# Fewer slots per expert rank, and one more expert in the one-tile form, in a mixture-of-experts decoder layer

## The chip, the cores and the metric

One core of one Trainium2 chip runs the whole layer in one launch. The metric is the device time of one execution in microseconds (us), as the median of repeated runs. All matrix products go through TensorE (PE), which multiplies a stationary block of at most 128 x 128 by a moving block of up to 512 columns; VectorE (DVE) and ScalarE (ACT) do the elementwise work, GpSimd (POOL) issues the gathers and scatters, and SyncE (SP) issues the other loads.

## The reference

A decoder layer on 1024 tokens of width 1024: gated and dilated attention mixers, a first LayerNorm that gives `h`, then a mixture of 32 experts of which each token takes its 4 best, and a second LayerNorm. The change concerns the mixture alone:

```python
logits = jnp.dot(hf, w_router) + b_router
top_vals, top_idx = lax.top_k(logits, TOP_K)          # 4 of 32
gates = jax.nn.softmax(top_vals, axis=-1)
# for the tokens xb of expert e:
g = jnp.minimum(xb @ w_gate[e] + b_gate[e], SWIGLU_LIMIT)
u = jnp.clip(xb @ w_up[e] + b_up[e], -SWIGLU_LIMIT, SWIGLU_LIMIT)
act = (u + 1.0) * (g * jax.nn.sigmoid(SWIGLU_ALPHA * g))
y[tok] += (act @ w_down[e] + b_down[e]) * gate
```

1024 tokens x 4 make 4096 token-expert pairs; how many of them an expert gets is known only once the router has run. Evaluated on the drawn inputs, the reference's router gives these counts, sorted: 225, 207, 188, 173, 171, 168, 163, 161, 148, 142, 139, 133, 126, 125, 125, 125, 122, 121, 119, 116, 113, 110, 109, 104, 100, 93, 93, 92, 90, 83, 62, 50.

## The kernel before, in words

The kernel computes mixers, first LayerNorm and router in a front stage of some 560 us. The router's part writes, for each expert, a list of tokens and gates into `table` (L632), and `rank()` sorts the experts by their count: rank 0 is the fullest expert, rank 31 the emptiest. The number of tokens is not known when the program is built, so each rank has a fixed number of **slots**, `CAPS[r]` (L42); slots that no token fills point at dummy rows. What does not fit is left over: `left_over()` (L128 to L165) counts, on the chip, the blocks of 128 tokens beyond the slots, and a loop behind the expert stage (L981 to L1039) runs one block per turn, with all twelve weight pieces of that expert loaded again. With no left-over block the loop's body does not run.

The expert stage takes the ranks in the order `ORDER` (L43): 0, 30, 15, 29, 1, 28, 14, 27, 2, 26, 13, 25, 3, 24, 12, 23 and so on to 7, 16, 8, 31. That is a full rank, one of 128 slots, one that is just over 128, one of 128 slots, four by four. Each expert has twelve weight pieces of 1 MB (128 x 2048 float32): eight for gate and up, four for down. `load` (L778) fetches a piece into one of `RAWS` = 5 buffers on SP's queue, ACT rounds it to the high part `wh` (L120) and DVE subtracts to get the low part `wl` in bfloat16 (L121), four pairs of which can stand ready (`SPLITS`). SP's order is written by hand: `pieces` (L795 to L799). The order of the other engines comes from the scheduler, which places each instruction when its inputs are expected.

For each piece PE multiplies high by high, high by low and low by high. There are two forms, by the number of slots n:

- **one-tile** (n of 128 or 64; `gate_up`, `tokens_still`, L821): the tokens are stationary (`xt`, `xbt`; `at`, `abt` for down), the weights move, 512 columns at a time. A piece takes 8 matmuls of 512 columns against `wh` and 4 against `wl`. The bias comes in by one matmul more (L844).
- **wide** (n over 128; `gate_up_wide`, `weights_still`, L830): the weights are stationary, and the tokens move. A piece takes 16 matmuls of 2n columns (`xw` or `aw`, high and low part side by side) and 16 of n columns (`xbw` or `abw`). ACT copies half of each result out of the bank (`sb`, L865 and L918), DVE adds the other half (`tw`, L867 and L919); for down, 16 transposes (L930) turn the result back.

Before an expert starts, `fetch` (L731) gathers its tokens into `xg` (L749, one transfer per 128 slots), and `prepare` (L763) transposes them on PE (L758) and splits them into `xt` and `xbt`, or `xw` and `xbw` (hi on ACT L120, lo on DVE L121, bfloat16 on ACT L760). The pool has one `xt` and one `xw`. The driver of the stage interleaves three things per expert: first half of gate and up, the down of the expert before, `prepare` of the next, second half:

```python
gu(b, 0, lambda: next(extra, None))
...
if last is not None:
    finish = down(last)
if nxt is not None:
    prepare(nxt)
gu(b, 1, lambda: (finish(), turn(b, 0)))
```

`turn` transposes the activations of a one-tile expert for its down product. The tail (L1047 to L1069) is the second LayerNorm.

Of the kernel before, what the change touches and what calls it, by code (L numbers as in the profile page):

```python
# [38 lines left out]
MAGIC = 0x5F3759DF  # L39


CAPS = [256, 240, 216, 208, 192, 184, 176, 168, 160, 152, 152, 144, 144, 140, 136, 136] + [128] * 15 + [64]  # L42
ORDER = [r for n in range(8) for r in (n, 30 - 2 * n, 15 - n, 29 - 2 * n)][:31] + [31]  # L43
MAXOV = 64
AHEAD = 2
# [11 lines left out]
def constants():  # L57
# [15 lines left out]
        "c_row": np.tile(np.arange(MAXOV, dtype=np.float32), (E, 1)),  # L73
        "c_caps": np.array(CAPS, np.float32)[:, None],
    }


def layer(tc, i, out):
# [630 lines left out]
    with (tc.tile_pool(name="c", bufs=1, reuse_waits="tile") as C,  # L709
# [20 lines left out]
        def fetch(r):  # L730
            b = Job()  # L731
            b.r, b.n = r, CAPS[r]
            b.wide = b.n > P
# [390 lines left out]
```

## Time and profile before

| | us |
|---|---|
| median of 3 runs (1987.77 to 1990.61) | 1988.18 |
| the profiled execution, its own time | 1989.86 |
| its span in the trace | 1988.0 |
| expert stage, first token transpose to last weight matmul | 568.5 to about 1944 |

The span is the time between the first and the last instruction; 1.86 us lie around it. "Busy" counts the time in which an engine executes; the chain of waits follows the work that ended last back from the end, and a window gives the busy time of each engine between two times. The TensorE clock that the chip granted (PEclk) is a share of full speed.

### The profile page before, as it was taken

The numbers are of one execution on the slowest core, as the hardware profiler recorded it, in microseconds if no ns is written. First come the engines' busy times: TensorE is split into PE (matmuls) and PEld (weight loads), VectorE is DVE, ScalarE is ACT, GpSimd is POOL, SyncE is SP. The second block draws the span as 40 slices with busy tenths as digits, with TensorE's granted clock in tenths as the row PEclk, the third lists the DMA queues.
The fourth block names the chain that finished last, engine by engine and source line by source line (L and its number), as shares of the span: only waits on it lengthen the run. The fifth ranks groups of instructions, "written<-read, shape, count | busy, mean of one in ns | idle before, by whom it ended". The sixth has DMA issues, their size and how long they took to land.

```text
span 1988.0 us, 32785 instructions
## 1 busy us (share of the span) xinstructions
PE 1864.2 (94%) x12402; PEld 1549.6 (78%) x12484; DVE 1563.0 (79%) x2195; ACT 1331.1 (67%) x1761; POOL 314.3 (16%) x202
## 2 busy tenths in 40 slices
PE   8999999989859999999999999999999999999981
PEld 7788786678747878887888888888888888888861
DVE  5754656667758887797879888888988988888895
ACT  5534525643247877687778778778877887877873
POOL 2111110213320111020112101011111110111110
PEclk9999999989979999999999999999999999999996
DMA  5111101242278898799789889999999999999884
GB/s 201 50 43 35 50 25 38 64 141 99 83 255 307 303 354 272 271 327 353 292 291 373 300 318 324 367 319 312 369 318 319 364 315 341 332 355 338 300 286 175
DMA packets 92657, 495.94 MB, mean 249 GB/s; under 512 B 20264, under 2 KB 20824, under 8 KB 43344
## 3 DMA queue, kind: packets, MB, share of 16 engines
q1 hardware_dynamic: 76128, 442.49, 60.3%
q0 software_dynamic: 14064, 42.92, 8.9%
q10 hardware_dynamic: 2304, 8.39, 1.1%
q8 instruction: 100, 1.64, 0.3%
q14 instruction: 61, 0.50, 0.1%
HBM read 457.04 MB, written 36.72 MB: 248 GB/s over the span
## 4 chain that ended last, share of the span: by engine, by line
PE 60%; DMA 4%; DVE 4%; issue 2%; ACT 2%; POOL 0%; SPq 0%; POOLq 0%; ACTq 0%; DVEq 0%
PE b L830 32%; PE b L821 23%; DMA raw<-in_w_moe 2%; PE b L758 2%; DVE wl L121 2%; PE b L930 1%; ACT wh L120 1%; DMA ys<-o,tg 1%; PE b L844 1%; DVE y L1069 1%; DVE y L1068 0%; DMA y<-ys 0%; DMA table<-pay,dst 0%; POOL table L632 0%; DMA xg<-hs,tg 0%
## 5 line engine op out<-in xcount | busy, mean ns | idle before, releaser
L121 DVE TENSOR_TENSOR wl<-raw,wh 128x2048 bf16<-128x2048 f32 (+1 forms) x385 | 874.9, 2284 | 151.1 <-ACT wh L120 149.8
L120 ACT ACTIVATE wh<-raw 128x2048 fp32r<-128x2048 f32 (+1 forms) x394 | 742.4, 1893 | 143.8 <-PE b L821 37.9
L830 PE MATMUL b<-xw,wh 128*128 128x272 f32 (+12 forms) x2048 | 352.4, 325 | 0.0
L830 PEld LDWEIGHTS b<-xw,wh 128*128 128x128 f32 x2048 | 319.1, 188 | 12.3
L821 PE MATMUL b<-wh,xt 128*128 128x512 f32 x992 | 267.6, 411 | 0.0
L830 PEld LDWEIGHTS <-wl 128*128 128x128 bf16 x3072 | 225.6, 98 | 19.0 <-issue 5.5
L821 PEld LDWEIGHTS b<-wh,xt 128*128 128x128 f32 x992 | 188.5, 190 | 47.5
L749 POOL DMA_INDIRECT xg<-hs,tg x48 | 78.7, 1639 | 791.1 <-PE b L758 353.4
L830 PE MATMUL b<-aw,wh 128*128 128x272 f32 (+12 forms) x1024 | 174.2, 325 | 0.0
L933 POOL DMA_INDIRECT ys<-o,tg x48 | 111.9, 2332 | 390.5 <-ACT o L931 152.8
L830 PE MATMUL b<-xbw,wl 128*128 128x136 bf16 (+12 forms) x2048 | 166.1, 239 | 0.7 <-DVE wl L121 0.7
L830 PEld LDWEIGHTS b<-aw,wh 128*128 128x128 f32 x1024 | 159.5, 188 | 6.2
L865 ACT ACTIVATE sb<-b 128x136 f32<-128x136 f32 (+12 forms) x256 | 78.2, 317 | 90.8 <-PE b L830 84.6
L821 PE MATMUL b<-wh,at 128*128 128x512 f32 x496 | 137.7, 419 | 0.0
L821 PE MATMUL b<-wl,xbt 128*128 128x512 bf16 x465 | 116.0, 380 | 2.9 <-issue 0.2
L821 PEld LDWEIGHTS b<-wh,at 128*128 128x128 f32 x496 | 93.1, 190 | 24.4 <-issue 0.6
L867 DVE SCALAR_TENSOR_TENSOR tw<-b,bias,sb 128x136 f32<-128x136 f32 (+12 forms) x256 | 91.5, 393 | 15.8 <-ACT sb L865 14.8
L821 PEld LDWEIGHTS <-xbt 128*128 128x128 bf16 x512 | 45.0, 98 | 63.2 <-issue 18.1
L830 PE MATMUL b<-abw,wl 128*128 128x136 bf16 (+12 forms) x1024 | 83.3, 239 | 2.5 <-DVE wl L121 2.5
L918 ACT ACTIVATE sb<-b 128x136 f32<-128x136 f32 (+12 forms) x128 | 38.5, 315 | 59.5 <-PE b L830 50.8
L124 PE MATMUL mm<-xh,wh 128*128 128x512 f32 x160 | 67.9, 424 | 10.3 <-DVE ks L359 6.9
L124 PE MATMUL mm<-vh,xh 128*128 128x256 f32 x256 | 72.6, 284 | 0.6 <-DVE ql L344 0.6
(364 smaller groups left out, 2842.1 us busy)
## 6 DMA issues: line engine op xcount, KB each, us to landing
raw<-in_w_moe SPq DMA_DIRECT2D x384, 1024.0 KB, 7.2
raw<-in_w_in SPq DMA_DIRECT2D x18, 512.0 KB, 3.6
raw<-in_w_out SPq DMA_DIRECT2D x8, 512.0 KB, 3.7
t<-in_x SPq DMA_DIRECT2D x8, 512.0 KB, 4.0
hs<-pt ACTq DMA_DIRECT2D x8, 512.0 KB, 3.1
ys<-pr ACTq DMA_DIRECT2D x8, 512.0 KB, 2.6
y<-ys SPq DMA_DIRECT2D x8, 512.0 KB, 5.7
out<-y SPq DMA_DIRECT2D x8, 512.0 KB, 2.6
```

The lines of the kernel that those rows point to most:

```text
L120: S.activation(hi, src, AF.Copy)
L121: by.tensor_tensor(lo, src, hi.bitcast(FT), op=OP.subtract)
L124: TE.matmul(o, ah, bh, start=start, stop=False)
L749: k.got = G.indirect_dma_start(out=k.x[:k.n], out_offset=None, in_=hs, in_offset=bass.IndirectOffsetOnAxis(ap=k.idx, axis=0))
L758: TE.transpose(tp[:, j], src(j), ident[:n, :n])
L821: TE.matmul(o, a, b, start=first and q == 0, stop=kq == 1 and q == len(every) - 1)
L830: TE.matmul(o, a, b, start=kq == 0 and j == 0, stop=kq == 1 and j == 3)
L844: TE.matmul(p, b.oh, bhl[:, m, half * 512:half * 512 + 512], start=True, stop=False)
L865: S.activation(x2[:, :n], p[f][:, n:2 * n], AF.Copy)
L867: V.scalar_tensor_tensor(t[:, f * n:f * n + n], p[f][:, :n], b.bias[:, c:c + 1], x2[:, :n], op0=OP.add, op1=OP.add)
L918: S.activation(x2[:, :n], p[:, n:2 * n], AF.Copy)
L933: G.indirect_dma_start(out=ys, out_offset=bass.IndirectOffsetOnAxis(ap=k.idx, axis=0), in_=k.o[:k.n], in_offset=None, compute_op=OP.add)
```

## The change

The list of slots per rank gets smaller numbers, and the sixteenth rank goes from 136 to 128, which by the test `b.n > P` makes it one-tile:

```diff
-CAPS = [256, 240, 216, 208, 192, 184, 176, 168, 160, 152, 152, 144, 144, 140, 136, 136] + [128] * 15 + [64]
+CAPS = [256, 220, 208, 196, 184, 176, 168, 164, 156, 148, 144, 140, 140, 136, 132, 128] + [128] * 15 + [64]
```

Nothing else differs. The scheduler then orders PE, ACT and DVE anew. Two places follow.

**ACT, second half of gate and up of a rank just over 128 slots.** `sb` is the copy out of the banks, `wh` the split of a weight piece, `aw` and `abw` the split of the activations, `t` the gate function of the one-tile expert around it. Before, rank 14, with 136 slots:

```order
L865 ACTIVATE sb<-b 128x136 x4
L120 ACTIVATE wh<-raw 128x2048 x3
L120 ACTIVATE aw<-tw 128x4x136
L880 ACTIVATE abw<-tw 128x544
L705 ACTIVATE t<-b 128x512
L120 ACTIVATE wh<-raw 128x2048 x3
L918 ACTIVATE sb<-b 128x136 x4
```

Now rank 14, with 132 slots:

```order
L865 ACTIVATE sb<-b 128x132
L120 ACTIVATE wh<-raw 128x2048 x2
L705 ACTIVATE t<-b 128x512
L120 ACTIVATE wh<-raw 128x2048
L120 ACTIVATE aw<-tw 128x4x132
L880 ACTIVATE abw<-tw 128x528
L120 ACTIVATE wh<-raw 128x2048 x2
L918 ACTIVATE sb<-b 128x132 x4
```

And now rank 13, with 136 slots:

```order
L865 ACTIVATE sb<-b 128x136 x4
L120 ACTIVATE wh<-raw 128x2048 x3
L120 ACTIVATE aw<-tw 128x4x136
L880 ACTIVATE abw<-tw 128x544
L705 ACTIVATE t<-b 128x512
L120 ACTIVATE wh<-raw 128x2048 x3
L918 ACTIVATE sb<-b 128x136 x4
```

At rank 14 the gate function and one weight split stand ahead of `aw`; at rank 13 the row order is the one that ranks 15 and 14 had before: three weight splits, `aw`, `abw`, and the gate function behind them.

**PE and DVE, from rank 30 (one-tile) to rank 15.** The last matmuls of rank 30's second half read `xt_5590`. On PE before, rank 15 follows with its own wide tile `xw_6101`, filled ahead:

```order
L821 MATMUL b_6207<-wl_6158,xbt_5591 128x512
L821 MATMUL b_6207<-wh_6157,xt_5590 128x512 x8
L830 MATMUL b_6266<-xw_6101,wh_6211 128x272 x4
L830 MATMUL b_6267<-xw_6101,wh_6211 128x272 x4
L830 MATMUL b_6268<-xw_6101,wh_6211 128x272 x4
L830 MATMUL b_6269<-xw_6101,wh_6211 128x272 x4
```

Now rank 15 is one-tile, and its tokens go into a second tenant of the one `xt` buffer, `xt_6096`:

```order
L821 MATMUL b_6188<-wh_6138,xt_5590 128x512 x8
L844 MATMUL b_6247<-bhl_5298,oh_6114 128x512
L149 MATMUL b_6285<-vc_5476,lt32_168 32x2
L844 MATMUL b_6294<-bhl_5298,oh_6114 128x512
L821 MATMUL b_6247<-wh_6192,xt_6096 128x512
L821 MATMUL b_6294<-wh_6251,xt_6096 128x512
L821 MATMUL b_6247<-wh_6192,xt_6096 128x512 x7
L821 MATMUL b_6294<-wh_6251,xt_6096 128x512
```

On DVE the split that fills it now stands there:

```order
L121 TENSOR_TENSOR at_5815<-b_6180,at_5815 128x4x128
L121 TENSOR_TENSOR wl_6252<-raw_6249,wh_6251 128x2048
L121 TENSOR_TENSOR xt_6096<-b_6098,xt_6096 128x4x128
L121 TENSOR_TENSOR xt_6096<-b_6106,xt_6096 128x4x128
L706 TENSOR_SCALAR t_6228<-b_6188 128x512
L121 TENSOR_TENSOR wl_6270<-raw_6267,wh_6269 128x2048
L707 SCALAR_TENSOR_TENSOR act_6226<-t_6227,t_6228 128x512
```

Between the last read of `xt_5590` and the first of `xt_6096` PE has two bias matmuls (and a small one of `left_over`); on DVE the two halves of `xt_6096` stand behind a weight split. The same pattern follows at the next passage, from rank 15 to rank 29. Before, the kernel had no passage from one 128-slot expert to another.

## Rows read from the trace of the kernel before

**Rows 1.** The page: busy time of each engine; the chain of waits by line.

```profile
PE 1864.2 (94%) x12402; PEld 1549.6 (78%) x12484; DVE 1563.0 (79%) x2195; ACT 1331.1 (67%) x1761; POOL 314.3 (16%) x202
...
PE b L830 32%; PE b L821 23%; DMA raw<-in_w_moe 2%; PE b L758 2%; DVE wl L121 2%; PE b L930 1%; ACT wh L120 1%; DMA ys<-o,tg 1%; PE b L844 1%; DVE y L1069 1%; DVE y L1068 0%; DMA y<-ys 0%; DMA table<-pay,dst 0%; POOL table L632 0%; DMA xg<-hs,tg 0%
```

**Rows 2.** Windows per pair: us; busy of PE, PEld, DVE, ACT, POOL; PEclk, DMA, GB/s.

```profile
652.10:729.20 77.10, 76.06 (x586) 63.79 (x589) 66.38 (x74) 62.76 (x75) 13.14 (x6) 1.00 0.94 329
729.20:834.30 105.10, 101.89 (x577) 82.56 (x580) 82.80 (x73) 72.37 (x82) 10.95 (x6) 0.98 0.82 288
834.30:911.40 77.10, 75.13 (x577) 63.33 (x580) 65.39 (x65) 62.59 (x75) 13.22 (x6) 1.00 0.95 327
911.40:1010.40 99.00, 96.09 (x579) 81.60 (x582) 81.21 (x73) 71.02 (x82) 10.97 (x6) 0.98 0.85 306
1010.40:1086.90 76.50, 76.17 (x578) 64.48 (x581) 68.02 (x66) 64.76 (x78) 16.20 (x6) 1.00 0.96 336
1086.90:1179.70 92.80, 92.32 (x579) 79.69 (x581) 77.50 (x72) 69.03 (x78) 9.51 (x6) 1.00 0.88 321
...
1347.00:1424.40 77.40, 77.08 (x579) 65.33 (x581) 68.41 (x66) 65.06 (x78) 11.56 (x6) 1.00 0.96 343
...
1676.20:1755.70 79.50, 79.22 (x579) 67.32 (x582) 70.08 (x66) 66.18 (x78) 12.75 (x6) 1.00 0.96 345
```

**Rows 3.** Groups by shape, TensorE: line, out<-in, shape, count; busy us, mean ns.

```profile
L830 PE MATMUL b<-xw,wh 128*128 128x272 f32 x256 | 35.4, 291 | 0.0
...
L830 PE MATMUL b<-xw,wh 128*128 128x480 f32 x128 | 29.0, 381 | 0.0
...
L830 PE MATMUL b<-xbw,wl 128*128 128x136 bf16 x256 | 16.5, 223 | 0.0
...
L830 PE MATMUL b<-xbw,wl 128*128 128x240 bf16 x128 | 13.8, 266 | 0.0
```

**Rows 4.** Windows, four weight pieces each: one-tile form, then wide form of 136.

```profile
618.70:630.50 11.80, 11.75 (x52) 7.86 (x52) 11.36 (x13) 10.07 (x8) 0.00 (x0) 1.00 0.63 239
667.60:679.90 12.30, 12.30 (x131) 11.97 (x131) 12.23 (x17) 10.01 (x12) 2.78 (x1) 1.00 0.96 296
```

**Rows 5.** Timeline of TensorE: start, us, what; sixteen token transposes.

```profile
729.15 1.81 PE L758 MATMUL b<-ident,xg 128*128 128x128 f32 x16
```

**Rows 6.** Waits of TensorE in the expert stage: total us, times, longest us.

```profile
PE b L844 <- DVE tw L919: 6.7, 4, 2.8
```

**Rows 7.** Timeline of ScalarE at rank 15: start, us, what [idle before <-releaser].

```profile
714.71 1.92 ACT L120 ACTIVATE wh<-raw 128x2048 fp32r<-128x2048 f32 x1 [2.79 <-DMA raw<-in_w_moe]
716.53 0.64 ACT L120 ACTIVATE aw<-tw 128x544 fp32r<-128x544 f32 x1
```

**Rows 8.** Windows just behind the wait after rank 15, and in a stretch of fast loads.

```profile
735.00:745.00 10.00, 9.78 (x49) 7.19 (x50) 7.83 (x7) 8.30 (x12) 0.95 (x1) 0.86 0.95 350
1083.00:1093.00 10.00, 9.71 (x82) 8.12 (x81) 10.00 (x15) 8.92 (x14) 0.17 (x1) 1.00 1.01 415
```

**Rows 9.** Waits of ScalarE for weight loads, ranks 15, 11, 10: us, times, longest.

```profile
ACT wh L120 <- DMA raw<-in_w_moe: 6.9, 4, 3.3
...
ACT wh L120 <- DMA raw<-in_w_moe: 3.4, 2, 2.8
...
ACT wh L120 <- DMA raw<-in_w_moe: 2.2, 1, 2.2
```

**Rows 10.** Groups by shape, VectorE, expert stage.

```profile
L121 DVE TENSOR_TENSOR wl<-raw,wh 128x2048 bf16<-128x2048 f32 x380 | 864.7, 2287 | 151.1 <-ACT wh L120 149.8
...
L121 DVE TENSOR_TENSOR xt<-b,xt 128x512 fp32r<-128x512 f32 x30 | 19.3, 680 | 0.0
```

**Rows 11.** Groups by shape, ScalarE, expert stage.

```profile
L120 ACT ACTIVATE xt<-b 128x512 fp32r<-128x512 f32 x30 | 16.4, 600 | 0.1
```

**Rows 12.** DMA issues of the whole run: count, KB each, median us to landing.

```profile
raw<-in_w_moe SPq DMA_DIRECT2D x384, 1024.0 KB, 7.2
...
ys<-o,tg POOLq DMA_INDIRECT x48, 9.9
```

## The prediction

> **What bounds the kernel now.** I read the page first [rows 1]: PE is busy for 94% of the span, and the chain of waits runs for 55% through the weight matmuls of the two forms, L830 (wide) and L821 (one-tile). A busy share says little of what one slot costs, so I went to windows. I cut the expert stage where the token transposes of a wide expert begin, so that each window holds one wide expert and one one-tile expert, twelve weight pieces of each [rows 2]; in order these are the pairs of ranks 15, 1, 14, 2, 13, 3, 11 and 9, with 136, 240, 136, 216, 140, 208, 144 and 152 slots. Three things are to be seen. First, in the pairs of 13, 3, 11 and 9 PE idles for 0.3 to 0.5 us in 76.5 to 92.8: PE's own work sets the time there. Second, the pairs of 15, 1, 14 and 2 have 1.0 to 3.2 us of idle PE; the list of PE's waits names DVE's `tw` in front of the bias matmul L844, 6.7 us in 4 waits, 2.8 the longest [rows 6]. Third, the DMA share is 0.94 to 0.96 in the pairs just over 128 slots and 0.82 to 0.88 in those of the full ranks. PE leads, the loads are close behind it, and DVE (66.4 of 77.1 us) and ACT come after.
>
> **Fewer slots in the wide form.** A wide piece has 16 matmuls of 2n columns and 16 of n. From 272 to 480 columns the mean goes from 291 to 381 ns, 0.433 ns per column; from 136 to 240 in bfloat16 from 223 to 266 ns, 0.413 ns [rows 3]. One slot costs 16 x (2 x 0.433 + 0.413) = 20.5 ns per piece, and 12 pieces make 0.2455 us. The windows agree: from 144 to 208 slots a pair grows from 77.4 to 92.8 us, 0.241 us per slot [rows 2]. Ranks 1 to 14 lose 20, 8, 12, 8, 8, 8, 4, 4, 4, 8, 4, 4, 4 and 4 slots, 100 in all: **-24.6 us**. The copies, adds and splits on ACT and DVE and the gathers of the second parts shrink too; I cost that at nothing, as PE's matmuls hide them. If that cover went, DVE with 66.4 us and ACT with 62.8 would still be below the 71 to 75 us that the shortest pair will have.
>
> **Rank 15 in the one-tile form.** Four pieces take 12.3 us wide with 136 slots and 11.8 us one-tile, biases included [rows 4]; three times that is 1.5 us. The wide expert also has 16 transposes of its result and 16 of its tokens against 8 and 8, and sixteen take 1.81 us [rows 5]. Together **-3.3 us**. A gather and a scatter of 8 rows on POOL's queue and a bias load on SP's go as well, all off the path.
>
> **The wait behind rank 15.** On the line of 0.2455 us per slot from rank 11's 77.4 us, a pair with 136 slots should take 75.4; it takes 77.1. Rank 1's pair should take 92.8 + 32 x 0.2455 = 100.7; it takes 105.1. So 1.7 + 4.4 = 6.1 us are lost at rank 15, and by the same sum 1.7 + 4.2 = 5.9 at rank 14. The pair of rank 13, 76.5 us, is on the line (76.4). Why: ACT's timeline at rank 15 shows a weight split that waits 2.79 us for its load and the split `aw` behind it [rows 7]; DVE then runs late, its `tw` comes behind two weight splits of 2.29 us, and PE waits for banks. Just behind that wait the granted clock of a 10 us window is 0.86, so part of it ran at 1.2 instead of 2.4 GHz [rows 8]; that is in the 4.4. With rank 15 one-tile there is no `aw` and no `tw` at that place: **-6.1 us**.
>
> **Ranks 14 and 13.** The loss stands where ACT has three weight splits, `aw`, and the gate function last, and not at rank 13, where the gate function and another split stood ahead. The change gives rank 14 the good row and rank 13, now at 136 slots, the bad one. So I let 5.9 us go at rank 14 and come back at rank 13: **0**.
>
> **The passages 30 to 15 and 15 to 29.** New: one `xt` buffer for two one-tile experts in a row. The split into it can't begin before PE has read the old tokens for the last time, and PE has only two bias matmuls meanwhile. No row shows this wait. With idle engines it is an ACT half and a DVE half, 0.60 + 0.68 = 1.3 us [rows 10, 11], less the two bias matmuls of 512 columns, 0.413 x 512 = 0.21 each [rows 3]: 0.9. On DVE a weight split of 2.29 us stands in front, which could begin just before: 2.29 + 0.68 - 0.42 = 2.5. Queued behind these are ACT's next weight split and DVE's gate chain, which have a piece or two of lead. I take 1.5 each, since ACT's part of the weight split ahead is free to run some two us before the passage: **+3.0 us**, ends 1.8 and 5.0.
>
> **The loads come nearer.** ACT waits 2.2 us for weight loads in rank 10's pair (152 slots), 3.4 in rank 11's (144), 6.9 in rank 15's [rows 9]: about 0.3 us per slot less. The ranks 9 to 14 lose 28 slots, so 8.2 us more of such waits. In rank 11's pair nothing of it reached PE, in rank 15's most; I take a quarter, **+2.0 us**, ends 0 and 8.2.
>
> **Sum.** -24.6 - 3.3 - 6.1 + 0 + 3.0 + 2.0 = -29.0 us. The profiled execution took 1989.86 us (span 1988.0 and 1.86 around it) and would take 1960.9; the median of the runs stands 1.68 lower, and I forecast **1959.2 us**.
>
> **Rivals.**
>
> *The loads set a floor under the pairs just over 128 slots.* If no pair gets under the shortest seen, 76.5 us, rank 15 gives 0.6, rank 14 0.6, rank 13 nothing, ranks 12 and 11 0.8 and 0.9, rank 10 2.0 and rank 9 1.0, together 5.9; the 72 slots of the ranks 1 to 8 give 17.7; the waits stay. That is -23.6: 1964.6 us. For it: the DMA share of 0.96. Against it: 10 us windows that moved 415 GB/s while PE stood at 9.7 of 10 [rows 8], where the best pair has a mean of 345. The Trainium skill (DMA: Bandwidth & Descriptors, section "Where 436 GB/s comes from") says that for transfers between HBM and SBUF the HBM side binds, at about 358 GB/s; by that, a pair's 27.4 MB (345 GB/s x 79.5 us) would need 76.6 us, the same floor. The 415 GB/s of the window speak against it.
>
> *The passages cost their upper end and the clock.* 2.5 us each and, as behind the 2.8 us wait, 14% of 10 us at the lower clock, 1.4 us: 2 x 3.9 = 7.8 in place of 3.0, 1964.0 us.
>
> *No wait at rank 13 either, and the loads keep up.* The gathers for rank 2 and rank 3 are smaller than those that followed ranks 15 and 14. Then 5.9 + 2.0 us more go: 1951.3 us.
>
> *Rank 14 keeps its wait though its row is better,* because PE comes even sooner there: 5.9 us less gain, 1965.1 us.
>
> *Slower: one expert overflows.* All rests on counts under the new slots. The reference's router gives 225, 207, 188, 173, 171, 168, 163, 161 for the ranks 0 to 7 against 256, 220, 208, 196, 184, 176, 168, 164; the tightest is rank 7 with 3 to spare, and the kernel rounds otherwise than the reference. Before, the loop's body did not run: all 384 loads of `w_moe` are the 12 x 32 of the experts [rows 12]. One block would load twelve pieces again with nothing beside it: at least 12 x 2.29 (DVE) + 7.2 + 9.9 = 44.5 us, at most 12 x (7.2 + 2.29) + 9.9 = 124 us [rows 10, 12]; I put it at 65, for three buffers overlap the loads: 2024 us. A single token over decides, since even 44.5 is more than 29.0. The same would hold if the inputs timed were of another drawing.
>
> **The numbers.** Forecast 0.50; the load floor 0.15; the passages 0.10; no waits 0.15; rank 14 keeps its wait 0.07; overflow 0.03. A range from 1951 to 1968 us takes in all of them but the overflow, and the ends of the unknown terms one at a time; some 0.15 may lie outside. A measurement of this kernel can tell about 0.2% (4 us) from no change: faster 0.96, within it 0.01, slower 0.03.
>
> **What would show it.** The pair of rank 3, now 196 slots, at 89.9 us and that of rank 10 (144) at 77.5 confirm the slot price. The window of rank 15's pair should be near 74.5 us (two one-tile experts of some 36 and the waits), with two PE waits of 0.9 to 2.5 us whose releaser is DVE's or ACT's `xt`; rank 1's pair near 95.7, without a wait for `tw`. At rank 13's pair and the one behind it a wait for `tw` of some 2.8 us and a dip of the clock; none at rank 14. No loads beyond 384. I would be wrong if the pairs just over 128 slots stopped at 76.5 us, if PE's waits for `wl` spread over the pairs of ranks 9 to 12, or if anything of L981 to L1039 ran.

## The result and the profile after

The changed kernel takes **1972.26 us** (median of 4 runs, 1969.78 to 1975.34) against 1987.97 for the kernel before, timed beside it: a ratio of 0.9913, 95% interval [0.9898, 0.9929]. That is 15.7 us faster where 29.0 were forecast, and 4.3 us above the upper end of the range, 1968. The profiled execution took 1973.29 us (span 1971.4), 12.4 more than the 1960.9 of the prediction's sum.

The page, busy time and the chain of waits by line, against [rows 1]:

```profile
PE 1844.5 (94%) x12232; PEld 1519.5 (77%) x12232; DVE 1548.3 (79%) x2169; ACT 1315.8 (67%) x1731; POOL 312.1 (16%) x200
...
PE b L830 28%; PE b L821 22%; DMA raw<-in_w_moe 4%; DVE wl L121 3%; DMA ys<-o,tg 3%; PE b L758 2%; ACT wh L120 2%; PE b L930 1%; PE b L844 1%; DVE y L1069 1%; DMA bias<-in_b_guT 0%; DVE y L1068 0%; DMA y<-ys 0%; POOL table L632 0%; DVE tw L867 0%
```

PE is 19.7 us less busy, and the loads of the weights have gone from 2% to 4% of the chain. The windows of the pairs of ranks 15, 1, 14, 2, 13, 3 and 11, cut and laid out as in [rows 2]:

```profile
651.90:721.90 70.00, 69.43 (x329) 47.24 (x328) 55.62 (x48) 51.66 (x46) 10.16 (x5) 1.00 0.93 316
721.90:828.10 106.20, 102.24 (x589) 84.56 (x588) 86.17 (x73) 75.08 (x81) 12.18 (x5) 0.97 0.84 309
828.10:908.40 80.30, 76.34 (x583) 64.23 (x581) 64.88 (x65) 62.06 (x75) 13.01 (x6) 0.98 0.91 316
908.40:1001.90 93.50, 92.53 (x582) 79.60 (x581) 79.86 (x74) 70.56 (x82) 9.52 (x6) 1.00 0.90 321
1001.90:1078.10 76.20, 75.55 (x582) 63.38 (x581) 64.45 (x62) 61.70 (x74) 13.19 (x6) 1.00 0.97 329
1078.10:1173.30 95.20, 91.52 (x583) 78.04 (x582) 80.21 (x76) 70.82 (x83) 11.80 (x6) 0.98 0.87 318
...
1338.80:1415.30 76.50, 76.41 (x582) 64.45 (x580) 67.58 (x66) 64.41 (x78) 12.01 (x6) 1.00 0.97 343
```

The first two have to be read as one. The token transposes that cut them come earlier within rank 15's down product than they do elsewhere, so two of its weight pieces lie in the second window (48 matmuls that read `at` there, 32 in the window of rank 2). Together they take 176.2 us, 182.2 before and 74.5 + 95.7 = 170.2 by the forecast. Rank 14's pair has become longer, 80.3 us with 132 slots where it took 77.1 with 136. Behind rank 13 the window of rank 3 has 3.7 us of idle PE and a clock of 0.98, as forecast. From rank 12 on the pairs lie within 1.2 us of the forecast.

What PE waited for in the expert stage, with `tw` first as in [rows 6] (the list also has 14.3 us at the first gather and 5.3 at the last expert, where the kernel before has 14.4 and 5.0):

```profile
PE b L844 <- DVE tw L919: 6.0, 5, 3.7
PE b L821 <- ACT abt L760: 5.7, 3, 4.0
...
PE b L830 <- DVE wl L121: 2.9, 3, 2.2
PE b L830 <- ACT abw L880: 1.7, 1, 1.7
```

The wait for `tw` has not gone; others have joined it. The longest of those shown lies at rank 1. TensorE's timeline there, and ScalarE's just before:

```profile
721.90 1.68 PE L758 MATMUL b<-ident,xg 128*128 128x128 f32 x16
727.53 1.89 PE L821 MATMUL b<-wl,abt 128*128 128x512 bf16 x4 [3.96 <-ACT abt L760]
```

```profile
712.12 1.91 ACT L120 ACTIVATE wh<-raw 128x2048 fp32r<-128x2048 f32 x1 [2.62 <-DMA raw<-in_w_moe]
...
715.40 1.91 ACT L120 ACTIVATE wh<-raw 128x2048 fp32r<-128x2048 f32 x1 [0.89 <-DMA raw<-in_w_moe]
720.36 1.92 ACT L120 ACTIVATE wh<-raw 128x2048 fp32r<-128x2048 f32 x1 [3.05 <-DMA raw<-in_w_moe]
722.18 0.57 ACT L120 ACTIVATE at<-b 128x512 fp32r<-128x512 f32 x1
722.65 1.90 ACT L120 ACTIVATE wh<-raw 128x2048 fp32r<-128x2048 f32 x1
725.09 1.91 ACT L120 ACTIVATE wh<-raw 128x2048 fp32r<-128x2048 f32 x1 [0.53 <-DMA raw<-in_w_moe]
726.90 0.58 ACT L760 ACTIVATE abt<-b 128x512 bf16<-128x512 f32 x1
```

ACT stands four times for a weight piece that has not landed, 7.1 us in all. Small work that PE needs, `at` and `abt`, is queued behind those splits, and PE stops for 3.96 us. The name in the list of waits is `abt`; what was late is the load (e7 and e10 below). Windows of 10 us around that stretch, columns as in [rows 8]:

```profile
660.00:670.00 10.00, 9.58 (x45) 6.34 (x44) 7.27 (x7) 8.92 (x13) 1.82 (x1) 1.00 0.98 286
670.00:680.00 10.00, 10.00 (x48) 6.63 (x47) 9.32 (x11) 7.59 (x8) 1.84 (x1) 1.00 0.97 287
680.00:690.00 10.00, 9.96 (x49) 6.59 (x48) 9.43 (x7) 6.18 (x6) 0.00 (x0) 1.00 1.00 417
...
720.00:730.00 10.00, 6.04 (x32) 4.00 (x31) 7.93 (x6) 8.30 (x9) 0.00 (x0) 0.81 0.98 389
730.00:740.00 10.00, 10.00 (x39) 6.59 (x38) 5.10 (x7) 7.12 (x9) 2.92 (x1) 0.85 0.65 230
```

Two things show. In 660 to 680, where POOL issues a scatter into `ys` in each window, the DMA engines are as busy as in 680 to 690 (share 0.97 to 1.00) and move 287 instead of 417 GB/s. And in the window of PE's stop and the one behind it the granted clock is 0.81 and 0.85: part of these 20 us ran at 1.2 GHz, the lower of the two levels.

At rank 14 it is DVE that stands, for the tiny load of the bias, 5.64 us, and then PE; the rows of DVE and of PE:

```profile
876.42 0.17 DVE L741 TENSOR_SCALAR bias<-bias 128x8 f32<-128x8 f32 x1 [5.64 <-DMA bias<-in_b_guT]
876.53 2.29 DVE L121 TENSOR_TENSOR wl<-raw,wh 128x2048 bf16<-128x2048 f32 x1
```

```profile
878.88 1.18 PE L830 MATMUL b<-xbw,wl 128*128 128x132 bf16 x16 [2.22 <-DVE wl L121]
```

### The profile page after: what moved, and what is told of

Same layout as the page of the kernel before. It is cut to its first block, busy times and chain, and to the rows that moved or that the text cites. A ratio compares the mean times of both kernels' runs of the same rounds, so it can differ in the third digit from the quotient of the medians.

```text
span 1971.4 us, 32268 instructions
## 1 busy us (share of the span) xinstructions
PE 1844.5 (94%) x12232; PEld 1519.5 (77%) x12232; DVE 1548.3 (79%) x2169; ACT 1315.8 (67%) x1731; POOL 312.1 (16%) x200
## 4 chain that ended last, share of the span: by engine, by line
PE 53%; DMA 8%; DVE 6%; issue 2%; ACT 2%; POOL 1%; SPq 0%; POOLq 0%; ACTq 0%; DVEq 0%
PE b L830 28%; PE b L821 22%; DMA raw<-in_w_moe 4%; DVE wl L121 3%; DMA ys<-o,tg 3%; PE b L758 2%; ACT wh L120 2%; PE b L930 1%; PE b L844 1%; DVE y L1069 1%; DMA bias<-in_b_guT 0%; DVE y L1068 0%; DMA y<-ys 0%; POOL table L632 0%; DVE tw L867 0%
## 5 line engine op out<-in xcount | busy, mean ns | idle before, releaser
L120 ACT ACTIVATE wh<-raw 128x2048 fp32r<-128x2048 f32 (+1 forms) x394 | 742.4, 1893 | 153.0 <-DMA raw<-in_w_moe 46.8
L830 PE MATMUL b<-xw,wh 128*128 128x280 f32 (+13 forms) x1920 | 326.4, 324 | 0.0
L830 PEld LDWEIGHTS b<-xw,wh 128*128 128x128 f32 x1920 | 297.8, 190 | 9.5
L821 PE MATMUL b<-wh,xt 128*128 128x512 f32 x1056 | 283.4, 409 | 0.1
L830 PEld LDWEIGHTS <-wl 128*128 128x128 bf16 x2880 | 209.0, 97 | 18.1 <-issue 5.1
L830 PE MATMUL b<-aw,wh 128*128 128x280 f32 (+13 forms) x960 | 160.0, 321 | 0.7 <-DVE aw L121 0.7
L830 PE MATMUL b<-xbw,wl 128*128 128x140 bf16 (+13 forms) x1920 | 153.4, 237 | 2.2 <-DVE wl L121 2.2
L865 ACT ACTIVATE sb<-b 128x140 f32<-128x140 f32 (+13 forms) x240 | 71.8, 313 | 79.1 <-PE b L830 72.4
L821 PEld LDWEIGHTS b<-wh,at 128*128 128x128 f32 x528 | 99.9, 192 | 26.2 <-issue 0.6
L867 DVE SCALAR_TENSOR_TENSOR tw<-b,bias,sb 128x140 f32<-128x140 f32 (+13 forms) x240 | 83.8, 389 | 11.3 <-ACT sb L865 10.6
L830 PE MATMUL b<-abw,wl 128*128 128x140 bf16 (+13 forms) x960 | 77.1, 237 | 2.4 <-ACT abw L880 1.7
L821 PE MATMUL b<-wl,abt 128*128 128x512 bf16 x272 | 72.4, 390 | 6.2 <-ACT abt L760 5.7
```

The source lines that it names most:

```text
L120: S.activation(hi, src, AF.Copy)
L821: TE.matmul(o, a, b, start=first and q == 0, stop=kq == 1 and q == len(every) - 1)
L830: TE.matmul(o, a, b, start=kq == 0 and j == 0, stop=kq == 1 and j == 3)
L865: S.activation(x2[:, :n], p[f][:, n:2 * n], AF.Copy)
L867: V.scalar_tensor_tensor(t[:, f * n:f * n + n], p[f][:, :n], b.bias[:, c:c + 1], x2[:, :n], op0=OP.add, op1=OP.add)
```

## The experiments

Each kernel's time is a median, with the ratio to the kernel before in the same batch (in 20, 7, 7, 11 and 9 runs of it its median was 1989.2, 1988.7, 1988.4, 1988.7 and 1990.1). From e5 on, theory A means late weight loads and theory B the order of the rows. The first four expectations name their theories otherwise, each in its own words; the theory B of e3 is not the later one.

**One part of the change alone (e1, e2).**

```diff
-CAPS = [256, 220, ... 136, 132, 128] + ...
+CAPS = [256, 220, ... 136, 132, 136] + ...      (e1: rank 15 stays wide)
-CAPS = [256, 240, ... 140, 136, 136] + ...
+CAPS = [256, 240, ... 140, 136, 128] + ...      (e2: from the kernel before, rank 15 alone)
```

> The changed kernel with rank 15 back at 136 slots, in the wide form; all other slots as changed. Theory L (the weight loads fall behind over three one-tile experts in a row, and what the one-tile form gains is given back as a wait in the pair of rank 1): the pair of rank 15 takes 77 us again (70.1 changed), the pair of rank 1 falls from 106 to 96 to 100 us, and the median is within 3 us of the changed kernel's 1972.3. Theory R (the one-tile form of rank 15 is worth its whole price, and the loss in the pair of rank 1 has another cause): the pair of rank 1 stays near 106 us and the median rises by 6 to 9 us, to 1978 to 1981.

> The kernel before with nothing but rank 15 at 128 slots, one-tile. Theory L: the pair of rank 15 falls from 77.1 to 70 us and the pair of rank 1 rises from 105.1 to 109 to 112 us: the median is 1984 to 1988. By the sum of the prediction (3.3 for the form, 6.1 for the wait, less 3.0 for the passages) it is 1981.6, with the pair of rank 1 at 100.7 us.

e1: 1977.51 us, 0.9946 [0.9927, 0.9965]. e2: 1987.81 us, 0.9991 [0.9976, 1.0005]. The slots alone give some 11 us of their 24.6, the form alone nothing that can be told from zero, though on top of the slots it gives some 5 us (1977.5 to 1972.3, in two batches). No theory has all its numbers: e1's time is near theory R's, but rank 1's pair takes 102.2 us, between the two; e2's time is in theory L's range, but rank 1's pair takes 106.1, short of its 109. In e2's profiled execution, at 1983.7 us one of its faster ones, the pairs of 15 and 1 fall from 182.2 to 176.8 us, and rank 2's rises from 99.0 to 100.1. In the changed kernel, with 20 slots less at rank 1, the same two pairs take 176.2. So twenty slots, 4.9 us of PE's work, brought 0.6 there. Something else than PE set the time.

**The bias on another engine, and another order (e3, e4).**

```diff
-                V.tensor_scalar(b.bias[:, 8:], b.bias[:, 8:], 1.0, None, op0=OP.add)
+                G.tensor_scalar(b.bias[:, 8:], b.bias[:, 8:], 1.0, None, op0=OP.add)
```

```diff
-ORDER = [r for n in range(8) for r in (n, 30 - 2 * n, 15 - n, 29 - 2 * n)][:31] + [31]
+ORDER = [0, 30, 15, 1, 29, 14, 28, 2, 27, 13, 26, 3, 25, ... 19, 9, 18, 16, 7, 17, 8, 31]
```

> The changed kernel with the addition of 1 to the bias of a wide expert (L741) on GpSimd in place of VectorE; the other rows of VectorE and all of ScalarE's and TensorE's stand as they did. Theory B (at rank 14 VectorE stands 5.6 us in front of this tiny addition, whose load comes late, and everything behind it in its queue is late): the pair of rank 14 falls from 80.2 to 75 to 76 us, no wait of VectorE for that load is left, and the median is 1966 to 1968. Rival (the weight loads are late there anyway): the pair stays at 79 to 80 us and the median at 1971 to 1973.

> The changed kernel with another order of the experts: rank 15 stands between rank 30 and rank 1, so that two one-tile experts in a row come twice (30, 15 and 18, 16) and three never; full ranks and those just over 128 slots still take turns. Theory L: the wait of 4.0 us and the slow clock behind it at rank 1 go, and the median is 1962 to 1967. Rival (a wait of this kind comes wherever ScalarE has a late weight split in front of the activations): it reappears at other places and the median stays within 3 us of 1972.3.

e3: 1975.32 us, 0.9927 [0.9895, 0.9959]; e4: 1969.37 us, 0.9907 [0.9881, 0.9933]: neither can be told from the changed kernel. In e3 DVE no longer waits for the bias, rank 14's pair falls by 2.0 us to 78.3, and rank 12's rises by 5.0 to 82.5. In e4 the wait for `abt` at rank 1 goes (1.7 us in all are left of 5.7), but `tw` (6.2), `wl` (2.9) and `abw` (2.6) stay. Both moved the loss; neither removed it.

**Loads and scatters taken away (e5 to e8).** e5 is the changed kernel again, for comparison. In e6 and e7 half of each weight piece is not loaded (the first half is used twice), in e6 for the six experts around ranks 1 and 14, in e7 for all but ranks 0 and 30. In e8 the scatters of the ranks 0 to 5 are left out. So e6 to e8 no longer compute the layer and tell about time alone. PE and ACT keep their rows in all of them.

```diff
-            w = SP.dma_start(out=raw, in_=i["w_moe"][ds(e, 1), c].rearrange("a p c -> p (a c)"))
+            w = SP.dma_start(out=raw[:, 0:2] if r in HALF else raw, in_=i["w_moe"][ds(e, 1), c][:, :, 0:1024 if r in HALF else 2048].rearrange("a p c -> p (a c)"))
...
-            split(h, l, raw)
+            split(h, l, raw) if r not in HALF else split(*(z.rearrange("p (a b) c -> p a (b c)", a=2) for z in (h, l)), raw[:, 0:2].rearrange("p b c -> p (b c)").unsqueeze(1).to_broadcast([P, 2, 1024]))
```

```diff
+                if b.r < 6:
+                    return
                 for k in b.parts:
                     G.indirect_dma_start(out=ys, ...
```

> The changed kernel itself, timed beside the three others of this batch, so that they can be compared with it on one chip. Both theories expect what it did before: some 1972 us, rank 1's pair near 106 us and rank 14's near 80, where the slot line gives 95.7 and 74.6. If these losses wander to other pairs from one profiled execution to the next, they depend on when loads land and not on the row order alone.

> Left out: the second half of every weight piece of the experts 15, 29, 1, 28, 14 and 27 is not loaded, the first half is read twice by the splits in its place. ACT and PE have the very same row order as the changed kernel, on DVE the bias add moves by one weight split at two places. Theory A (weight loads land late beside gathers and scatters, and the in-order queues hand the delay on): the loss of 10.4 us in rank 1's pair and of 5.6 in rank 14's goes, so 106.2 becomes about 96 and 80.2 about 75, the total falls by some 15 us to about 1957, and the loss at rank 13 or 3 stays. Theory B (the order of rows on ACT and DVE makes PE wait, loads or not): the two pairs stay within 2 us of 106 and 80 and the total within 4 us of the changed kernel.

> Left out: as before, now for all experts but 0 and 30, so that weight loads take half of their traffic nearly everywhere. Theory A: besides the 15 us at ranks 1 and 14, the waits for tw behind rank 13 (4 us) and what the loads took from the later pairs (1 us each in the pairs of 15 to 9) go: 1948 to 1953 us, with no wait of PE over 2 us between the first and the last expert. Theory B: within 4 us of the changed kernel; the wait for tw behind rank 13, which stands at the row order with the gate function behind aw, stays at 3 to 4 us in any case if the row order makes it.

> Left out: the scatter-add of the results of the ranks 0 to 5 (11 transfers of up to 128 rows of 4 KB, read, add and write), the order on PE, ACT and DVE is unchanged. If theory A holds and the scatters of the full ranks are the traffic that delays the weight loads, the pairs of ranks 1 and 14 lose 5 to 12 of their 16 us of delay and the total falls to 1958 to 1967. If the weights alone fill the queues there, the pairs stay within 2 us and the total within 4 us of the changed kernel. Theory B expects no change either.

e5: 1974.33 us (0.9923), with the losses in the same places: rank 1's pair 106.4 us, rank 14's 80.2. e6: 1963.46 us, 0.9866 [0.9841, 0.9891], 10.9 below e5. e7: 1952.81 us, 0.9823 [0.9807, 0.9839], 21.5 below. e8: 1963.47 us, 0.9874 [0.9858, 0.9891], 10.9 below. The windows of the pairs of ranks 15, 1, 14 and 3 in e7:

```profile
652.40:722.50 70.10, 69.01 (x324) 47.31 (x329) 59.23 (x52) 54.93 (x49) 10.92 (x5) 1.00 0.74 218
722.50:822.30 99.80, 99.29 (x585) 83.18 (x588) 82.78 (x70) 71.71 (x78) 10.70 (x5) 1.00 0.56 165
822.30:896.70 74.40, 74.15 (x578) 62.59 (x581) 66.78 (x66) 64.11 (x78) 14.68 (x6) 1.00 0.67 196
...
1064.10:1153.90 89.80, 89.56 (x579) 77.44 (x582) 76.52 (x72) 68.11 (x79) 11.97 (x6) 1.00 0.59 172
```

With the rows of PE and ACT unchanged and half the loads, the losses are gone, the wait behind rank 13 too: rank 14's pair takes 74.4 us (74.5 on the slot line), rank 3's 89.8 (89.9 without a wait), 15 and 1 together 169.9 (170.2). ACT's waits for weight loads in the expert stage fall from 46.8 us to 4.1. Theory B had expected no change. e6 misses its figure of 15: it recovers 6.4 us at rank 1, 5.9 at rank 14 and 1.1 at rank 2, and my 10.4 at rank 1 had been read from that window alone, with the two pieces of rank 15 in it. And e8, the pairs of ranks 1 and 14:

```profile
720.00:826.00 106.00, 101.49 (x586) 84.51 (x589) 86.54 (x73) 74.96 (x81) 12.01 (x5) 0.97 0.84 310
826.00:900.40 74.40, 74.15 (x578) 62.59 (x581) 65.32 (x65) 62.65 (x75) 8.46 (x4) 1.00 0.91 330
```

Without the scatters rank 14's loss is gone with all weights loaded; rank 1's is not, nor rank 3's (95.5 us). At rank 1 three one-tile experts (30, 15, 29) follow each other, which only the change brings about, and e4, which parts them, lost the wait for `abt`.

**One load buffer more (e9 to e12).** Six buffers find room beside a rank 0 of 240 slots (the fullest expert has 225 tokens), so e9 prices that alone.

```diff
-CAPS = [256, 220, 208, ...
+CAPS = [240, 220, 208, ...      (e9 to e12)
-RAWS = 5
+RAWS = 6                        (e10 to e12; e11 with the order of e4, e12 with the bias add of e3 too)
```

> The changed kernel with rank 0 at 240 slots instead of 256, which makes room for one more buffer in the next run. All theories expect the slot price alone: 16 x 0.2455 = 3.9 us off the changed kernel (1972 to 1974), with the losses at ranks 1, 14 and 3 where they were: about 1969.

> As the run before, with six load buffers instead of five; PE and ACT keep their row order, on DVE the bias add moves by a weight split at some places. Theory A (the loads of a stretch come a few us too late, and what PE stands still for is what the lead of five raw and four split pieces does not cover): one piece more is 2.5 to 3 us of lead at the start of each tight stretch, the waits for tw, abt and wl of 2 to 4 us shrink to under 1.5 us or go, and with them the stretches at half the clock; 8 to 16 us below the run before, 1953 to 1961. Rival (the queues are too slow over the whole of the groups of ranks 15 to 3, so any lead is used up before): less than 4 us below the run before.

> As the run before, with the order in which rank 1 stands between the one-tile experts 15 and 29 (0, 30, 15, 1, 29, 14, 28, 2 and so on), so that no three one-tile experts follow each other. If the stretch of three one-tile experts is what used up the lead before rank 1, and the sixth buffer alone did not cover it, this takes 2 to 6 us more; if the sixth buffer already covered it, it is within 3 us of the run before.

> As the run before, with the add on the bias tile (L741) on GpSimd, so that a late bias load holds up no weight split on DVE. Theory A: 0 to 4 us less than the run before, since a wait of DVE of 5.6 us stood before rank 14 in the changed kernel; if late weight loads rule in any case, no difference.

e9: 1970.74 us (0.9913), where about 1969 was expected. e10: **1953.14 us** (1951.75 to 1955.63), 0.9822 [0.9806, 0.9839], 17.6 below e9 and a little more than theory A had expected. e11: 1953.55 (0.9817), e12: 1954.29 (0.9834): with the sixth buffer neither the order nor the bias add makes a difference. e10's windows of ranks 1, 14, 13 and 3:

```profile
718.90:818.80 99.90, 99.80 (x590) 83.22 (x589) 82.80 (x70) 71.79 (x78) 9.77 (x5) 1.00 0.87 322
818.80:897.50 78.70, 76.08 (x581) 63.94 (x580) 65.02 (x65) 62.46 (x75) 14.27 (x6) 0.98 0.87 308
...
990.50:1065.70 75.20, 75.20 (x582) 63.37 (x581) 68.06 (x66) 64.21 (x78) 14.02 (x6) 1.00 0.95 338
1065.70:1155.50 89.80, 89.80 (x581) 77.34 (x580) 76.39 (x72) 68.23 (x78) 9.09 (x6) 1.00 0.91 333
```

PE's waits for `wl`, `abt` and `tw` come to 2.6, 1.7 and 1.1 us, none over 1.5, and ACT's for weight loads to 13.0. With every byte loaded, 99.9 and 89.8 us are what e7 had with half of them. One loss is left, 4.3 us at rank 14.

**The kernel before with six buffers (e14).**

```diff
-CAPS = [256, 240, 216, ...
+CAPS = [240, 240, 216, ...
-RAWS = 5
+RAWS = 6
```

> The kernel before with rank 0 at 240 and six load buffers, the slots of all other ranks as they were. Theory A (the losses of 12 us that the prediction put down to the order of ACT's rows behind ranks 15 and 14 were late loads as well): 1988.2 - 3.9 - 8 to 12 = 1972 to 1976, without a wait for tw of over 1.5 us, although the rows keep the order with the gate function behind aw. Rival (the row order): 3.9 us less than before, 1984, and waits for tw of 2 to 3 us. The difference to the run with six buffers under the new slots is then what the slots and the one-tile form give when loads are in time: 28 us by the prediction's first two terms if both have no waits.

1973.15 us (1970.77 to 1974.37), 0.9919 [0.9896, 0.9942]: 15.5 us faster than the kernel before, about as much as the whole change, and 4.0 of it rank 0's slots. Ranks 15, 1, 14 and 2, against the first four of [rows 2]:

```profile
648.40:724.50 76.10, 76.10 (x590) 63.75 (x589) 69.05 (x75) 64.83 (x78) 13.62 (x6) 1.00 0.95 341
724.50:825.00 100.50, 100.48 (x582) 81.67 (x581) 79.64 (x72) 70.38 (x78) 10.57 (x6) 1.00 0.82 297
825.00:900.20 75.20, 75.20 (x581) 63.32 (x580) 68.13 (x66) 64.53 (x78) 14.43 (x6) 1.00 0.94 336
900.20:995.00 94.80, 94.80 (x583) 80.53 (x582) 78.18 (x72) 69.30 (x78) 9.42 (x6) 1.00 0.86 320
```

PE has no idle time in them and no wait for `tw` is left in its list, though ACT still has three weight splits, `aw` and the gate function last at ranks 15 and 14. ScalarE at rank 15, against [rows 7]:

```profile
706.51 1.92 ACT L120 ACTIVATE wh<-raw 128x2048 fp32r<-128x2048 f32 x1 [1.69 <-PE b L821]
708.34 0.64 ACT L120 ACTIVATE aw<-tw 128x544 fp32r<-128x544 f32 x1
708.88 0.64 ACT L880 ACTIVATE abw<-tw 128x544 bf16<-128x544 f32 x1
709.43 0.57 ACT L705 ACTIVATE t<-b 128x512 f32<-128x512 f32 x1
```

The rows are the same; the split in front of `aw` now waits for PE and not for its load, and ACT's waits for weight loads fall from 31.6 us to 4.3. The waits of the kernel before were late loads, not the order of the rows.

**The loss left at rank 14 (e13, e15, e16).** e13 is e10 with the bias add on GpSimd; e15 is e10 with 136 slots at rank 14, which gives ACT the rows of rank 13 there; e16 has both.

```diff
-CAPS = [240, 220, ... 140, 140, 136, 132, 128] + ...
+CAPS = [240, 220, ... 140, 140, 136, 136, 128] + ...      (e15, e16)
```

> Six load buffers, rank 0 at 240, the order of the changed kernel, and the add on the bias tile on GpSimd; only DVE's rows of L741 move. With six buffers one loss is left in the groups of ranks 15 to 3: DVE waits 6.96 us for the bias load of rank 14 and PE then 2.6 us for wl, with a stretch at half the clock behind it; rank 14's pair takes 78.7 us, 74.4 without such waits. If the tiny load in front of the weight splits is what stands there, the pair falls to 74.4 to 75.5 and the total by some 4 us to about 1949. If the weight loads are late there in any case, the wait moves to another row and the total stays within 2 us of 1953.

> As the run with six buffers (e10), with rank 14 at 136 slots instead of 132: ACT's rows there are then those of rank 13, three weight splits, aw, abw, and the gate function behind them, where at 132 slots the gate function and a weight split stand ahead of aw. The prediction's step on row order expects the wait at rank 14 to grow (5.9 us dearer). Theory A expects the four slots alone, 1.0 us dearer, if the late bias load on DVE makes the loss there (rank 14's pair at 79.7). If the row with a weight split ahead of aw is the harmful one when a load is late, the pair falls to 75.4 to 77 and the total by 2 to 4 us to 1949 to 1951.

> The run before with the bias add on GpSimd. Whichever of the late bias load and the row with a weight split ahead of aw stands at rank 14, neither is left: its pair takes 75.2 to 76 us and the total is 1948 to 1950. If it stays near 79, weight loads are late there whatever the rows.

e13: 1951.08 us, 0.9815 [0.9788, 0.9841]; e15: 1955.17, 0.9821 [0.9801, 0.9841]; e16: 1955.82, 0.9830 [0.9804, 0.9855]. None can be told from e10. The pairs of ranks 14 and 2 together: 171.7 us in e10, 172.3 in e13 (PE now waits 4.1 us for `abw`), 174.5 in e15 (2.9 us for `tw`), 174.1 in e16, 166.7 in e7; the four slots more of e15 and e16 make 1.0 of theirs. So 5.0 to 6.8 us are lost in all four, and neither the bias load nor the row order is the cause, alone or together; they choose which operation PE is seen waiting for. The loads are late there with six buffers too (ACT waits for them for 12.2 us in e16, 13.0 in e10).

## Why the prediction was wrong

**The step that failed is the one on the waits**: "Why: ACT's timeline at rank 15 shows a weight split that waits 2.79 us for its load and the split `aw` behind it", followed by "the loss stands where ACT has three weight splits, `aw`, and the gate function last". I had the load in [rows 7] and put the loss down to the rows around it. So I let 6.1 us go with rank 15's `aw`, let 5.9 move from rank 14 to rank 13, and asked 2.0 for loads that come nearer. The forecast of the wait behind rank 13 came true, and for a reason that was wrong: it goes in e10 with the same rows, and e14 keeps the rows at ranks 15 and 14 and has no wait there.

**The term that was mis-sized** is that of the late loads. The kernel before lost 13.9 us to them: e14's span is 17.9 us shorter, of which rank 0's 16 slots make 4.0. The changed kernel lost 21.5, by e7 (spans 1971.4 and 1949.9). I had 12.0 before and 5.9 + 2.0 = 7.9 after. A gain of 4.1 from them was really a loss of 7.6, 11.7 of the 12.4 us that the sum is off. The two yardsticks are not the same (a sixth buffer before, half the loads after); by the medians the sixth buffer gave back 11.5 us in the kernel before and 17.6 in the changed one, which keeps 4.3 more at rank 14, so by either measure the loss rose by some 8 to 10 us. The lead of the five raw and four split pieces was the resource, as the sixth buffer shows, and I read the rise so that each slot removed shortens the time in which the lead is refilled; ACT's waits for weight loads in the expert stage rose from 31.6 to 46.8 us. I asked a quarter of 8.2 for the ranks 9 to 14 and nothing for ranks 15 and 1, where three experts of the shortest PE time now follow each other, and did not ask what else was on the queues there.

**The slot price held**: 0.2455 us. Rank 10's pair (144 slots) took 77.4 us, forecast 77.5. With six buffers in both kernels the pairs of 13 and 3 fell from 168.8 to 165.0 us, 3.8 for 16 slots, forecast 3.9.

**Form and passages** (-3.3 and +3.0). With loads in time the pairs of 15 and 1 went from 176.6 (e14) to 169.9 us (e7); less 4.9 for the slots that is -1.8, forecast -0.3 (-1.5 by e10's 170.2). So the passages cost nothing that shows, and the form gave about half of its 3.3; where the rest went no run shows. At the passage from rank 30 to rank 15 no wait of PE shows, nor at the one from 15 to 29. TensorE, ScalarE and VectorE at the first:

```profile
667.48 0.50 PE L844 MATMUL b<-bhl,oh 128*128 128x512 f32 x1
667.85 2.90 PE L821 MATMUL b<-wh,xt 128*128 128x512 f32 x10
```

```profile
667.20 1.09 ACT L120 ACTIVATE xt<-b 128x512 fp32r<-128x512 f32 x2 [1.08 <-PE b L821]
```

```profile
667.88 1.28 DVE L121 TENSOR_TENSOR xt<-b,xt 128x512 fp32r<-128x512 f32 x2
```

PE reads the new `xt` at 667.85, when only ACT's first half can be done and DVE has not begun: the buffer is handed over in pieces, and the two bias matmuls cover ACT's half. I had added a DVE half and a weight split in front. The weight split ahead on DVE had ended in time. I had also put each bias matmul at 0.21 us, the slope of [rows 3] without its constant part; in the trace of the kernel before one takes 0.45 (28.8 us for 64), so the cover was twice what I took.

**The rivals.** The range missed by 4 us because it took the ends of the unknown terms one at a time, while late loads stood behind three of them: the wait at rank 15, the waits at ranks 14 and 13, and the loads' own. That rank 14 keeps its wait came true: 5.9 us are lost there (80.3 us against 74.4 in e6 and e8). I had given it a chance of 0.07, and it accounts for 5.9 of the 12.4 us. The floor of 76.5 us under a pair was not there: rank 13's takes 75.2 in e10 with all its loads, and rank 14's 74.4 in e8. The Trainium skill (DMA: Bandwidth & Descriptors, section "Where 436 GB/s comes from") puts the bind of such transfers at about 358 GB/s on the HBM side; 417 GB/s in the window from 680 us, on the one core that runs, speak against it here. Yet the rival named the right resource: not a floor per pair, but a lead that runs out over several. No token overflowed: 384 weight loads, as before (rank 15, 125 tokens in 128 slots, was as tight as rank 7).

**With loads in time** the change is worth 20.0 us (1973.15 to 1953.14, six buffers on both sides), against 27.9 of the first two terms; 4.3 of the difference stand at rank 14, where loads are late still, and 1.8 at ranks 15 and 1, where slots and form make 8.2 and the pairs fell by 6.4 (176.6 to 170.2). What delays the loads at rank 14 I did not settle: of what shares the queues, only the scatters were tried, with five buffers.

## What to carry to other kernels

When a wait names an operation on an in-order engine, look at what that engine itself waited for just before; if it is a load, moving rows may only rename the wait, as in e3 and e13. Before counting a gain from less work on the leading engine, ask what the lead of the loads was before and how much of it the shorter work leaves, over a run of several stages and with gathers and scatters on the same queues. Halving the loads with all rows kept shows in one run what late loads cost, and one more buffer can be worth more than the work removed (here 17.6 us, and 15.7 for the whole change).

## What the runs showed of the hardware

Scatters that add into memory go with a lower rate of all transfers, their own bytes included: 286 and 287 GB/s in two windows with one scatter issued in each, 417 in the next with none, at about the same share of busy DMA engines (0.97 to 1.00). By the queues' own counts in these two windows the scatters took 27% of the DMA engines' time for 1.02 MB and the loads 70% for 4.69 MB; in the next the loads took 98% of half that time for 4.15 MB. By these figures, an estimate, a scattered byte took 2.2 times the engine time of a byte loaded alone, and a byte loaded beside scatters 1.26 times. In the same stretch of e8, without the two scatters, the five weight loads landed in a median of 4.8 us, 6.8 with them; leaving out the scatters of six ranks took 10.9 us. And a stop of PE costs more than its length. In the changed kernel the windows of ranks 1, 14 and 3, the three in which PE stood for 2 to 4 us at a time, have a clock of 0.97 to 0.98. At rank 1 PE was busy for 102.24 us against 99.29 in e7, 2.95 more for the same work, behind a stop of 3.96.
